# A Mamba-2 output stage with one activation table, its products moved to ScalarE and its exp rows made ahead, and the memory of the later stages laid anew

## Chip, cores and metric

One core of one Trainium2 chip runs the whole layer as one program. The metric is the device time of one execution in microseconds (us). PE is TensorE, DVE VectorE, ACT ScalarE, POOL GpSimd, SP SyncE, which here only issues transfers.

## What is computed

One layer of a diffusion backbone over 1024 latent and 256 context tokens of width 1024, in float32: a normalised input is projected once, and its columns feed latent attention (8 heads), a bidirectional Mamba-2 state-space branch (2048 inner columns, 32 heads of 64, 4 groups of 8 heads, state 128, chunks of 128 tokens), and two gates; then come the merged output projection and a SwiGLU feed-forward network. What the change touches is the end of the Mamba-2 branch:

```
def finish(yf, yb, x_, z_):
    y = (yf + yb + d * x_).reshape(b, -1, D_INNER)
    return rmsnorm(y * jax.nn.silu(z_), w_ssd_norm)
```

`yf` and `yb` are the forward and the backward scan. With cs the running sum of the decay's logarithms, C, B and x of a chunk, and S the state that enters it, each direction gives for a chunk exp(cs) (C S) + ((C B^T) masked, times exp(cs_l - cs_m), times dt) x. The gates are sigmoids of other projected columns.

## The kernel before

Matrix products are made to float32 accuracy: each operand is split into a high part, rounded by ACT, and the rest, by DVE's subtraction, and a 128x512 tile takes three products (L145, L146, L147). The stages are: preparation, the projection of x, B and C with its convolution (the xBC stage, 140 to 535 us in the profile), the end of the reverse scan, the **SSD output stage** (about 590 to 1139 us), attention (to 1608 us), and the output stage with the feed-forward network (to the end). A scheduler orders the instructions of each engine from the program's order, its pools of buffers and its dependences.

The SSD output stage (L693 to L830) works on 32 chunks, 8 for each of 4 groups. For chunk i `load_in` (L697) brings B and C (`bc`) and the rows of cs of both directions, broadcast over the partitions (`cf`, `cb`); `load_out` (L706) the backward state (`sbt`), `ra` with x, and `xz` with d x and silu(z). `in_a` makes the exponent: POOL subtracts a column from `cf` (L721), DVE takes for each of 8 heads the minimum with `cb` less a column (L733), ACT the exp (L735); PE makes C B^T (`pg`), DVE masks it for both directions (`gw`, L726, L727); ACT also makes exp(cs) in four instructions, the upper and the lower half of the partitions apart, as heads lie (`ef`, L742). `in_b` weighs the masks with dt: POOL for the backward direction (`um`, L752), DVE adds the forward one head by head (L757) and multiplies (L758). `out_a` multiplies the states with C (`py`, L771), weighs them (L772), makes the next state (`pst`, L775, and DVE's sum `sn`, L498 in `chunk_state`), adds the directions and d x on POOL (L779, L780), and multiplies with x (`pyd`, L787); `out_b` adds (L794) and multiplies with silu(z) (L795), `chunk_end` stores y (L800). `in_a` runs two chunks ahead of `out_a`, `in_b` one.

Between these, PE is filled with the projection of z and the gates, `zg_steps` (L637 to L665): 32 blocks of 16 steps, each step three products; four blocks come before the stage. 12 steps stand at the stage's start, 13 between the chunks' products (ZG_A to ZG_E), the rest at its end. ACT takes Silu or Sigmoid of a finished block (L655), so that it changes its activation table between these and exp. The weights of each block are split by ACT (L116) and DVE (L117).

Attention's pools are opened over the memory of the stage before, so that its first loads (`ckvh`, `ckvl`, L849) wait for the last users of their place. The output stage begins with y2, the gated y: 16 half tiles are loaded, ACT or DVE rounds them (`load_half`, L1046 to L1054), `sq_add` (L1062) sums their squares on ACT and POOL, and each is split in place, so that the loads hold the buffers of the split (`u`, NU = 80 of 128x512).

Of the kernel before, what the change touches and what calls it, by code (L numbers as in the profile page):

```python
# [54 lines left out]
NU, NW, NE = 80, 20, 4  # L55
# [4 lines left out]
def hybrid_layer(ctx, tc, ins, out):  # L60
# [398 lines left out]
    V.tensor_copy(cs_t[:, :, 0:32], pcf)  # L459
    V.tensor_copy(cs_t[:, :, 32:64], pcb)  # L460
    for q in range(2):
# [77 lines left out]
    with ExitStack() as es:  # L539
# [101 lines left out]
        def zg_steps(pp_tile, zt_tile):  # L641
# [3 lines left out]
            fn = AF.Silu if b < 16 else AF.Sigmoid  # L645
            zt = None
            for hf in range(2):
# [914 lines left out]
```

## Time and profile before

| | us |
|---|---|
| Median of three runs (lowest, highest) | 2654.67 (2651.73, 2655.33) |
| Profiled execution | 2657.29 |
| its span in the trace | 2655.5 |
| SSD output stage, 598 to 1100 | 502 |
| PE busy in the span | 2488.9 (94%) |
| DVE, ACT, POOL busy in the span | 1772.9, 1189.3, 978.9 |

The profiled execution is one run; its span runs from the first to the last instruction. The mean granted clock of PE is 0.975 of full speed. A busy share over the whole span mixes stages with different limits; the rows below are therefore taken from single stages.

### The profile page before, as it was taken

Reading aid. Unit: us, or ns where it says so; the run is one execution under the profiler, and the core shown is the slowest. Engines: PE = TensorE matmul, PEld = TensorE weight load, DVE = VectorE, ACT = ScalarE, POOL = GpSimd, SP = SyncE. Lnnn points to the kernel's source line nnn. Section 1 sums busy time; section 2 is a strip of 40 time slices with the busy share of each in tenths; the row PEclk is TensorE's granted clock in tenths of the full one; section 3 lists DMA queues with packets and bytes.
Section 4 is the critical chain, followed back from the end, with each engine's and each line's share of the span. In section 5 each row is a group of like instructions: output and inputs, shape, how many; then the busy total and the mean of one; then the engine's idle time right before and its main releaser. Section 6 shows DMA issues by size and latency. Waiting matters only on the chain. (4 is left out here: it accounts for less than half of the span.)

```text
span 2655.5 us, 35014 instructions
## 1 busy us (share of the span) xinstructions
PE 2488.9 (94%) x12716; PEld 2039.1 (77%) x12716; DVE 1772.9 (67%) x2715; ACT 1189.3 (45%) x2036; POOL 978.9 (37%) x800
## 2 busy tenths in 40 slices
PE   8999999987888888879999998999999999999998
PEld 5778787766667767768888886888887778888887
DVE  3766767758888888646776866254449655555876
ACT  5633333325656566435666664232235332234443
POOL 1312333346666666533443545271011423222000
PEclk9999999999999999989999997999999999999999
DMA  8455664456766666420000112243351323226713
GB/s 304 131 159 185 210 193 135 151 182 226 232 208 215 209 226 209 146 99 11 17 17 9 43 46 90 84 155 112 126 184 37 120 84 117 106 80 239 278 38 123
DMA packets 241373, 367.41 MB, mean 138 GB/s; under 512 B 17584, under 2 KB 127280, under 8 KB 241200
## 3 DMA queue, kind: packets, MB, share of 16 engines
q1 hardware_dynamic: 206128, 323.22, 36.6%
q10 hardware_dynamic: 35072, 41.95, 4.6%
q8 instruction: 100, 1.64, 0.3%
q14 instruction: 73, 0.60, 0.1%
HBM read 262.87 MB, written 102.24 MB: 137 GB/s over the span
## 5 line engine op out<-in xcount | busy, mean ns | idle before, releaser
L145 PE MATMUL pp<-hTh,whi 128*128 128x512 f32 x896 | 373.2, 417 | 0.0
L145 PE MATMUL pse<-hi 128*128 128x512 f32 x924 | 361.4, 392 | 9.7 <-DVE c L1301 5.3
L147 PE MATMUL pse<-hi,lo 128*128 128x512 f32 x924 | 361.3, 391 | 0.8 <-DVE lo L1036 0.7
L146 PE MATMUL pse<-lo,hi 128*128 128x512 f32 x924 | 361.2, 391 | 0.0
L146 PE MATMUL pp<-hTl,whi 128*128 128x512 f32 x896 | 351.6, 392 | 0.0
L147 PE MATMUL pp<-hTh,wlo 128*128 128x512 f32 x896 | 351.4, 392 | 0.0
L1036 DVE TENSOR_TENSOR lo<-wr,hi 128x512 fp32r<-128x512 f32 x231 | 167.9, 740 | 134.8 <-ACT hi L1035 134.7
L1035 ACT ACTIVATE hi<-wr 128x512 fp32r<-128x512 f32 x231 | 141.0, 627 | 254.4 <-PE pse L146 60.2
L117 DVE TENSOR_TENSOR wlo<-wraw,whi 128x1024 fp32r<-128x1024 f32 (+1 forms) x106 | 153.6, 1450 | 109.3 <-ACT whi L116 102.7
L953 POOL TENSOR_TENSOR prob<-prob,mx 128x1280 f32<-128x1280 f32 x64 | 149.2, 2332 | 209.5 <-DVE mx L952 87.3
L145 PEld LDWEIGHTS pse<-hi 128*128 128x128 f32 x924 | 174.2, 189 | 51.3 <-DVE c L1301 8.7
L146 PE MATMUL pse<-lo,whi 128*128 128x512 f32 x512 | 204.6, 400 | 9.2 <-DVE lo L1053 9.0
L145 PEld LDWEIGHTS pp<-hTh,whi 128*128 128x128 f32 x896 | 169.8, 190 | 51.8 <-issue 18.0
L147 PEld LDWEIGHTS pse<-hi,lo 128*128 128x128 f32 x924 | 174.3, 189 | 38.1 <-DVE lo L1036 2.1
L145 PE MATMUL pse<-hi,whi 128*128 128x512 f32 x512 | 202.1, 397 | 0.9 <-ACT hi L1052 0.5
L147 PE MATMUL pse<-hi,wlo 128*128 128x512 f32 x512 | 202.6, 396 | 0.0
L146 PEld LDWEIGHTS pse<-lo,hi 128*128 128x128 f32 x924 | 174.1, 188 | 36.9 <-DVE lo L1036 1.0
L146 PEld LDWEIGHTS pp<-hTl,whi 128*128 128x128 f32 x896 | 169.8, 189 | 40.2 <-issue 7.8
L733 DVE SCALAR_TENSOR_TENSOR xm<-cb,cs_t,xm 128x128 f32<-128x128 f32 x256 | 180.2, 747 | 26.5 <-POOL xm L721 24.9
L147 PEld LDWEIGHTS pp<-hTh,wlo 128*128 128x128 f32 x896 | 169.0, 189 | 37.2 <-issue 0.3
L116 ACT ACTIVATE whi<-wraw 128x1024 fp32r<-128x1024 f32 (+1 forms) x106 | 111.0, 1048 | 169.5 <-PE pse L146 115.0
L564 DVE SCALAR_TENSOR_TENSOR sv<-u,cols,sv 128x1284 f32<-128x1284 f32 (+1 forms) x96 | 159.3, 1660 | 1.4
(340 smaller groups left out, 5729.2 us busy)
## 6 DMA issues: line engine op xcount, KB each, us to landing
wr<-w_ffn SPq DMA_DIRECT2D x88, 256.0 KB, 3.8
tb<-bt_d SPq DMA_DIRECT2D x77, 256.0 KB, 5.3
wa<-w_ada ACTq DMA_DIRECT2D x64, 256.0 KB, 5.2
wraw<-w_zg SPq DMA_DIRECT2D x32, 512.0 KB, 4.4
cf<-csT_d SPq DMA_DIRECT2D x32, 512.0 KB, 5.4
cb<-csT_d SPq DMA_DIRECT2D x32, 512.0 KB, 3.9
xz<-rb_d SPq DMA_DIRECT2D x32, 512.0 KB, 4.4
ra_d<-xt SPq DMA_DIRECT2D x20, 640.0 KB, 5.2
```

The lines of the kernel that those rows point to most:

```text
L116: S.activation(hi, raw, AF.Copy)
L117: V.tensor_tensor(lo, raw, hi, ALU.subtract)
L145: PE.matmul(ps, lhsT=sh, rhs=mh, start=first, stop=False, skip_group_check=more)
L146: PE.matmul(ps, lhsT=sh, rhs=ml, start=False, stop=False, skip_group_check=more)
L147: PE.matmul(ps, lhsT=sl, rhs=mh, start=False, stop=last, skip_group_check=more)
L564: V.scalar_tensor_tensor(sv[:, 0:nn], u[:, j : j + nn], cw(j), sv[:, 0:nn], ALU.mult, ALU.add)
L733: V.scalar_tensor_tensor(xm[:, a, :], cb[:, h, :], csb[:, h : h + 1], xm[:, a, :], ALU.subtract, ALU.min)
L953: GP.tensor_tensor(pr, pr, mx[:, 6:7].to_broadcast([P, TA]), ALU.mult)
L1035: S.activation(hi, src, AF.Copy)
L1036: V.tensor_tensor(lo, src, hi, ALU.subtract)
```

## The change

The SSD output stage needs one activation table: silu and sigmoid are made from Tanh, which lies in the table of Exp, with a second ACT pass, and for z with a multiply on DVE. Exp(cs) is made once in the xBC stage, stored in HBM, and loaded for each chunk as two broadcasts of 64 partitions (`ld_ef`). The subtraction of `xm` goes from POOL to 8 ACT instructions with a column as bias (cs is kept negated in the forward half for that), the weights `um` from POOL and DVE to 16 ACT instructions with a column as scale and two DVE sums. The store of y comes one chunk later, behind the next loads. The pools of attention are laid in another order; the output stage gets a pool of 16 buffers of its own (`r`), laid first, for raw loads and short-lived tiles, NU goes from 80 to 71, and a smaller scratch for DMA makes room. The splits of the first y2 tiles are no longer in place, and their squares come after them.

```diff
-NU, NW, NE = 80, 20, 4
+NU, NR, NW, NE = 71, 16, 20, 4
...
-    V.tensor_copy(cs_t[:, :, 0:32], pcf)
+    V.tensor_scalar(cs_t[:, :, 0:32], pcf, -1.0, None, ALU.mult)
...
+        ec = p1.tile([64, NT, P], F32, name="ec")
+        def exp_rows(i):
+            if i == 2:
+                SY.dma_start(ec, csT_d.rearrange("c h l -> h c l"))
+            elif i == 4:
+                S.activation(ec, ec, AF.Exp)
+            elif i in (6, 7):
+                di = i - 6
+                for g in range(G):
+                    for v in range(2):
+                        h0 = 32 * di + 8 * g + v
+                        SY.dma_start(ecT_d[:, g, v, di].rearrange("c a l -> a c l"), ec[h0 : h0 + 7 : 2])
...
-                S.activation(zt[:, hs(hf)], pp, fn)
+                S.activation(zt[:, hs(hf)], pp, AF.Tanh, scale=0.5)
+                S.activation(zt[:, hs(hf)], zt[:, hs(hf)], AF.Identity, scale=0.5, bias=halfc)
+                if b < 16:
+                    V.tensor_tensor(zt[:, hs(hf)], zt[:, hs(hf)], pp, ALU.mult)
...
+        def ld_ef(g, t):
+            ef = p2.tile([P, 2, 4, P], F32, tag="ef", name="ef", bufs=3)
+            for v in range(2):
+                SY.dma_start(ef[64 * v : 64 * v + 64], ecT_d[t, g, v].partition_broadcast(64))
+            return ef
...
+            c["ef"] = ld_ef(g, t)
...
-            csf, csb = h8(cs_t, 0, g, t), h8(cs_t, 1, g, t)
+            ncf, csb = h8(cs_t, 0, g, t), h8(cs_t, 1, g, t)
             c["xm"] = [p2.tile([P, 4, P], F32, tag="xm", name="xm", bufs=6) for _ in range(2)]
-            for hh in range(2):
-                h4 = slice(4 * hh, 4 * hh + 4)
-                GP.tensor_tensor(c["xm"][hh], cf[:, h4, :], bc3(csf[:, h4], P), ALU.subtract)
+            for h in range(R):
+                S.activation(c["xm"][h // 4][:, h % 4, :], cf[:, h, :], AF.Identity, bias=ncf[:, h : h + 1])
...
-            ef = p2.tile([P, 2, 2, 2, P], F32, tag="ef", name="ef", bufs=3)
-            for di, c_ in enumerate((cf, cb)):
-                c5 = c_.rearrange("p (a j v) l -> p a j v l", j=2, v=2)
-                for v in range(2):
-                    rs = slice(64 * v, 64 * v + 64)
-                    S.activation(ef[rs, :, di], c5[rs, :, :, v, :], AF.Exp)
-            c["ef"] = ef
...
-            ums = []
             for hh in range(2):
-                um = p2.tile([P, 4, P], F32, tag="um", name="um", bufs=3)
-                GP.tensor_tensor(um, gw[:, 1:2, :].to_broadcast([P, 4, P]), bc3(dtb_[:, 4 * hh : 4 * hh + 4], P), ALU.mult)
-                ums.append(um)
-            for um, xm, hh in zip(ums, c["xm"], range(2)):
+                xm = c["xm"][hh]
+                um, ub = [p2.tile([P, 4, P], F32, tag=n_, name=n_, bufs=2) for n_ in ("um", "ub")]
                 for a in range(4):
                     h = 4 * hh + a
-                    V.scalar_tensor_tensor(um[:, a, :], gw[:, 0, :], dtf[:, h : h + 1], um[:, a, :], ALU.mult, ALU.add)
+                    S.activation(um[:, a, :], gw[:, 0, :], AF.Copy, scale=dtf[:, h : h + 1])
+                    S.activation(ub[:, a, :], gw[:, 1, :], AF.Copy, scale=dtb_[:, h : h + 1])
+                V.tensor_tensor(um, um, ub, ALU.add)
                 V.tensor_tensor(xm, xm, um, ALU.mult)
...
-            chunk_end(i, out_b(i, c))
+            y_i = out_b(i, c)
             if i + 2 < n:
                 load_out(i + 2, cs[i + 2])
             if i + 3 < n:
                 cs[i + 3] = load_in(i + 3)
+            if i > 0:
+                chunk_end(i - 1, y_p)
+            y_p = y_i
             steps(zg, ZG_C)
+        chunk_end(n - 1, y_p)
...
-        pf = pool("pd0", es=es)
-        p3 = pool("pd1", es=es)
-        pv_ = pool("pd2", es=es)
-        pe_ = pool("pd3", es=es)
+        pe_ = pool("pd0", es=es)
+        pf = pool("pd1", es=es)
+        p3 = pool("pd2", es=es)
+        pv_ = pool("pd3", es=es)
...
+        pr4 = pool("per", es=es)
...
+        def split2(raw, fast=False):
+            hi, lo = u("hi", F32R), u("lo", F32R)
             if fast:
-                V.tensor_copy(hi, lo)
+                V.tensor_copy(hi, raw)
             else:
-                S.activation(hi, lo, AF.Copy)
-            V.tensor_tensor(lr, lo, hi, ALU.subtract)
-            return hi, lr
+                S.activation(hi, raw, AF.Copy)
+            V.tensor_tensor(lo, raw, hi, ALU.subtract)
+            return hi, lo
...
-        y2 = [[load_y2(k, 0, raw[k])] for k in range(8)]
+        y2 = [[split2(raw[k])] for k in range(8)]
         for k in range(8):
-            y2[k].append(load_y2(k, 1, raw[8 + k]))
+            y2[k].append(split2(raw[8 + k]))
...
+                if d == 0:
+                    for k in range(8):
+                        sq_add(ssy, hf, raw[8 * hf + k])
...
-    nc = _bacc.Bacc("TRN2", target_bir_lowering=False, num_devices=1)
+    nc = _bacc.Bacc("TRN2", target_bir_lowering=False, num_devices=1, dynamic_dma_scratch_size=1024)
```

The order of DVE in the middle of the third group, one chunk, before (`gw` are the two masked products, `sn` the state, `ef` the weighted states):

```order
L733 SCALAR_TENSOR_TENSOR xm<-cb,cs_t,xm 128x128 x4
L726 TENSOR_TENSOR gw<-pg,msk 128x128
L727 TENSOR_TENSOR gw<-pg,msk 128x128
L733 SCALAR_TENSOR_TENSOR xm<-cb,cs_t,xm 128x128 x2
L757 SCALAR_TENSOR_TENSOR um<-gw,dt_t,um 128x128 x5
L758 TENSOR_TENSOR xm<-xm,um 128x512
L757 SCALAR_TENSOR_TENSOR um<-gw,dt_t,um 128x128 x3
L733 SCALAR_TENSOR_TENSOR xm<-cb,cs_t,xm 128x128
L758 TENSOR_TENSOR xm<-xm,um 128x512
L772 TENSOR_TENSOR ef<-ef,py 128x512 x2
L733 SCALAR_TENSOR_TENSOR xm<-cb,cs_t,xm 128x128
L498 TENSOR_TENSOR sn<-sn,pst 128x512
```

and with the change:

```order
L758 TENSOR_TENSOR gw<-pg,msk 128x128
L759 TENSOR_TENSOR gw<-pg,msk 128x128
L765 SCALAR_TENSOR_TENSOR xm<-cb,cs_t,xm 128x128 x8
L121 TENSOR_TENSOR wlo<-wraw,whi 128x1024
L796 TENSOR_TENSOR ef<-ef,py 128x2x256 x2
L780 TENSOR_TENSOR um<-um,ub 128x512
L504 TENSOR_TENSOR sn<-sn,pst 128x512
L781 TENSOR_TENSOR xm<-xm,um 128x512
```

The eight small sums of `um` are gone, two large ones stand in their place, and the eight minima stand together.

The order of PE at the start of the last group, where `sf` is that group's first state (`pp` are products of z and the gates), before:

```order
L146 MATMUL pp_8666<-hTl_247,whi 128x512
L147 MATMUL pp_8666<-hTh_239,wlo 128x512
L771 MATMUL py<-bc,sf 128x128 x2
L771 MATMUL py<-bc,sbt 128x128 x2
L771 MATMUL py<-bc,sf 128x128 x2
L771 MATMUL py<-bc,sbt 128x128 x2
L775 MATMUL pst<-xw,ra 128x512
L145 MATMUL pp_8666<-hTh_240,whi 128x512
```

and with the change:

```order
L151 MATMUL pp_9287<-hTh_239,wlo 128x512
L149 MATMUL pp_9287<-hTh_240,whi 128x512
L150 MATMUL pp_9287<-hTl_248,whi 128x512
L794 MATMUL py<-bc,sf 128x128 x2
L794 MATMUL py<-bc,sbt 128x128 x2
L794 MATMUL py<-bc,sf 128x128 x2
L794 MATMUL py<-bc,sbt 128x128 x2
L799 MATMUL pst<-xw,ra 128x512
L151 MATMUL pp_9287<-hTh_240,wlo 128x512
L794 MATMUL py<-bc,sn 128x128 x2
L794 MATMUL py<-bc,sbt 128x128 x2
L794 MATMUL py<-bc,sn 128x128 x2
```

The first `py` of the group (on `sf`) is followed, with the change, by that of its second chunk (on `sn`), with no product of `pp` between; the products that stood there have moved ahead of the first one.

The order of ACT at the start of the output stage, before:

```order
L979 ACTIVATE ob<-po 128x256
L980 DMA oT_d_134<-ob 128x256
L1066 ACTIVATE sqa<-lo 128x512
L1069 ACTIVATE sq<-lo 128x512
L1052 ACTIVATE hi<-lo 128x512
L1069 ACTIVATE sq<-lo 128x512 x2
L1052 ACTIVATE hi<-lo 128x512
```

and with the change:

```order
L1007 ACTIVATE ob<-po 128x256
L1008 DMA oT_d_135<-ob 128x256
L1083 ACTIVATE hi<-raw 128x512 x16
L1155 ACTIVATE acc<-pse 128x512
L1102 ACTIVATE sqa<-raw 128x512
L1105 ACTIVATE sq<-raw 128x512 x8
```

All 16 roundings (`hi`) now stand ahead of the squares (`sqa`, `sq`), which before stood between them.

## Rows read from the trace of the kernel before

**Rows 1.** Windows, 598 to 1100 us. Columns: window, its us, busy us (instructions) of PE, PEld, DVE, ACT, POOL, clock, DMA share, GB/s.

```profile
598.00:1100.00 502.00, 427.46 (x2268) 336.90 (x2267) 435.25 (x767) 293.86 (x359) 321.67 (x269) 0.94 0.64 212
```

**Rows 2.** One tile's instructions, yt: the stores of y on SP.

```profile
L800 SPq DMA_DIRECT2D y_d<-yt x32: 370/370/371, 632.5 to 1122.6; - x32
```

**Rows 3.** Timeline of PE, 919 to 928 us. Columns: start us, us, instruction.

```profile
919.86 0.68 PE L771 MATMUL py<-bc,sn 128*128 128x128 f32 x4 [0.93 <-DVE sn L498]
...
922.18 0.79 PE L145 MATMUL pp<-hTh,whi 128*128 128x512 f32 x1
922.81 0.39 PE L146 MATMUL pp<-hTl,whi 128*128 128x512 f32 x1
923.03 0.39 PE L147 MATMUL pp<-hTh,wlo 128*128 128x512 f32 x1
...
926.77 1.09 PE L787 MATMUL pyd<-xm,ra 128*64 128x128 f32 x16
```

**Rows 4.** Waits, 598 to 1100 us. Columns: us in total, times, longest.

```profile
ACT xm L735 <- DVE xm L733: 133.7, 44, 7.3
...
PE py L771 <- DVE sn L498: 56.4, 24, 4.7
...
DVE xm L733 <- POOL xm L721: 24.9, 21, 1.3
```

**Rows 5.** Timeline of DVE, 907 to 917 us.

```profile
907.85 2.94 DVE L733 SCALAR_TENSOR_TENSOR xm<-cb,cs_t,xm 128x128 f32<-128x128 f32 x4 [1.31 <-POOL xm L721]
...
916.71 0.34 DVE L733 SCALAR_TENSOR_TENSOR xm<-cb,cs_t,xm 128x128 f32<-128x128 f32 x1
```

**Rows 6.** Groups of instructions, 598 to 1100 us: count | busy us, mean ns | idle before, releaser.

```profile
L733 DVE SCALAR_TENSOR_TENSOR xm<-cb,cs_t,xm 128x128 f32<-128x128 f32 x256 | 180.2, 747 | 26.5 <-POOL xm L721 24.9 <-DMA cb<-csT_d 1.6
...
L757 DVE SCALAR_TENSOR_TENSOR um<-gw,dt_t,um 128x128 f32<-128x128 f32 x248 | 105.1, 481 | 0.0
...
L758 DVE TENSOR_TENSOR xm<-xm,um 128x512 f32<-128x512 f32 x62 | 43.8, 706 | 0.0
...
L721 POOL TENSOR_TENSOR xm<-cf,cs_t 128x512 f32<-128x512 f32 x64 | 71.2, 1132 | 17.2 <-DMA cf<-csT_d 17.2
...
L752 POOL TENSOR_TENSOR um<-gw,dt_t 128x512 f32<-128x512 f32 x62 | 65.7, 1079 | 31.3 <-DVE gw L726 27.8 <-DVE xm L758 3.5
```

**Rows 7.** The same view: ScalarE.

```profile
L655 ACT ACT_TABLE_LOAD x47 | 60.3, 1283 | 3.8 <-DMA rb_d<-zt 3.0
...
L742 ACT ACT_TABLE_LOAD x30 | 38.5, 1283 | 7.4 <-DMA cf<-csT_d 4.2 <-ACT zt L655 2.8
...
L735 ACT ACT_TABLE_LOAD x18 | 23.1, 1283 | 50.0 <-DVE xm L733 49.9
...
L742 ACT ACTIVATE ef<-cf 64x512 f32<-64x512 f32 x64 | 40.2, 628 | 9.2 <-DVE yt L794 8.6
```

**Rows 8.** Timeline of ScalarE, 88.9 to 90.2 us: small shapes.

```profile
88.99 0.30 ACT L317 ACTIVATE junkb<-mt 128x128 f32<-128x128 f32 x1
89.19 0.19 ACT L317 ACTIVATION_READ_ACCUMULATOR junkb<-mt 128x1 f32 x1
...
90.18 0.55 ACT L262 ACTIVATE hf<-pt,modt,a 128x256 f32<-128x256 f32 x1
```

**Rows 9.** The page's part 2: bytes moved in 40 slices of 66.4 us.

```profile
GB/s 304 131 159 185 210 193 135 151 182 226 232 208 215 209 226 209 146 99 11 17 17 9 43 46 90 84 155 112 126 184 37 120 84 117 106 80 239 278 38 123
```

**Rows 10.** Timeline of PE, 1139 to 1144 us.

```profile
1143.19 0.79 PE L146 MATMUL pk<-ckvl,whi 128*128 128x512 f32 x1 [3.91 <-DMA ckvl<-mq_dl]
```

**Rows 11.** Windows, 1610 to 1640 us.

```profile
1610.00:1640.00 30.00, 23.06 (x51) 13.89 (x52) 26.91 (x23) 12.44 (x24) 20.88 (x14) 0.54 0.25 88
```

**Rows 12.** Timeline of DVE and POOL from 1609 us.

```profile
1609.68 0.69 DVE L1053 TENSOR_TENSOR lo<-lo,hi 128x512 fp32r<-128x512 f32 x1 [1.19 <-ACT sqa L1066]
...
1611.73 3.45 DVE L1053 TENSOR_TENSOR lo<-lo,hi 128x512 fp32r<-128x512 f32 x2
...
1610.25 21.82 POOL L1070 TENSOR_TENSOR sqa<-sqa,sq 128x512 f32<-128x512 f32 x14 [8.14 <-ACT sq L1069]
```

More of the change, by code (lines that the diff above doesn't have):

```diff
@@ L102, in hybrid_layer @@
     V.memset(epsc, EPS)
+    halfc = cp.tile([P, 1], F32, name="halfc")
+    V.memset(halfc, 0.5)
     modt = cp.tile([P, 6, KD, 2], F32, name="modt")
@@ L465, in hybrid_layer @@
         S.activation(dec_t[:, sl5], ptt, AF.Exp)
-        V.tensor_tensor(wst_t[:, sl5], ptt, cs_t[:, sl5], ALU.subtract)
+        V.tensor_tensor(wst_t[:, sl5, 0:32], ptt[:, :, 0:32], cs_t[:, sl5, 0:32], ALU.add)
+        V.tensor_tensor(wst_t[:, sl5, 32:64], ptt[:, :, 32:64], cs_t[:, sl5, 32:64], ALU.subtract)
     S.activation(wst_t, wst_t, AF.Exp)
@@ L473, in hybrid_layer @@
         cst = bp.tile([64, 4, P], F32, tag="cst", name="cst", bufs=1)
-        V.tensor_copy(cst, pct)
+        V.tensor_scalar(cst[0:32], pct[0:32], -1.0, None, ALU.mult)
+        V.tensor_copy(cst[32:64], pct[32:64])
         SY.dma_start(csT_d[q * 4 : q * 4 + 4].rearrange("c h l -> h c l"), cst)
@@ L626, in hybrid_layer @@
             pps = xbc_mm(b)
+            exp_rows(i)
             steps(scan, 1)
@@ L771, in out_a @@
                         PE.matmul(py[:, di, j, :], lhsT=st_[:, jj * P : jj * P + P], rhs=cT, start=True, stop=True)
-                V.tensor_tensor(ef[:, hh], ef[:, hh], py, ALU.mult)
+                e_ = ef[:, :, 2 * hh : 2 * hh + 2, :]
+                V.tensor_tensor(e_, e_, py, ALU.mult)
             if t < NT - 1:
@@ L776, in out_a @@
                 sf = chunk_state(g, t, 0, sf, pst)
-            e0, e1 = ef[:, :, 0], ef[:, :, 1]
+            e0, e1 = ef[:, 0], ef[:, 1]
             steps(zg, ZG_D)
             GP.tensor_tensor(e0, e0, e1, ALU.add)
-            GP.tensor_tensor(e0, e0, xz[:, 0:512].rearrange("p (a j l) -> p a j l", j=2, l=P), ALU.add)
+            GP.tensor_tensor(e0, e0, xz[:, 0:512].rearrange("p (a l) -> p a l", l=P), ALU.add)
             pyd = ps2.tile([P, 4, P], F32, tag="pyd", name="pyd", bufs=1)
@@ L792, in out_b @@
         def out_b(i, c):
-            yt = p2.tile([P, 2, 2, P], F32, tag="yt", name="yt", bufs=2)
-            V.tensor_tensor(yt, c["ef"][:, :, 0], c["pyd"].rearrange("p (a j) l -> p a j l", j=2), ALU.add)
-            GP.tensor_tensor(yt, yt, c["xz"][:, R_SZ - R_XD : RB_N - R_XD].rearrange("p (a j l) -> p a j l", j=2, l=P), ALU.mult)
-            return yt.rearrange("p a j l -> p (a j) l")
+            yt = p2.tile([P, 4, P], F32, tag="yt", name="yt", bufs=3)
+            V.tensor_tensor(yt, c["ef"][:, 0], c["pyd"], ALU.add)
+            GP.tensor_tensor(yt, yt, c["xz"][:, R_SZ - R_XD : RB_N - R_XD].rearrange("p (a l) -> p a l", l=P), ALU.mult)
+            return yt
         def chunk_end(i, yt):
@@ L1028, in u, with r @@
             return p4.tile([P, 512], dt, tag="u", name=name, bufs=NU)
+        def r(name, dt=F32):
+            return pr4.tile([P, 512], dt, tag="r", name=name, bufs=NR)
         def ps():
@@ L1039, in fetch, with load_half, load_y2 @@
         def fetch(src, hf):
-            lr = u("lo", F32R)
-            SY.dma_start(lr.bitcast(F32), src[:, hs(hf)])
-            return lr
-        def load_half(src, hf, sums=None, fast=False, lr=None):
-            lr = lr if lr is not None else fetch(src, hf)
-            hi, lo = u("hi", F32R), lr.bitcast(F32)
-            if sums is not None:
-                sq_add(sums, hf, lo)
+            t_ = r("raw")
+            SY.dma_start(t_, src[:, hs(hf)])
+            return t_
+        def split2(raw, fast=False):
+            hi, lo = u("hi", F32R), u("lo", F32R)
             if fast:
-                V.tensor_copy(hi, lo)
+                V.tensor_copy(hi, raw)
             else:
-                S.activation(hi, lo, AF.Copy)
-            V.tensor_tensor(lr, lo, hi, ALU.subtract)
-            return hi, lr
+                S.activation(hi, raw, AF.Copy)
+            V.tensor_tensor(lo, raw, hi, ALU.subtract)
+            return hi, lo
+        def load_half(src, hf):
+            return split2(fetch(src, hf))
         def y2_src(k):
             return y2_d[k // 4][k % 4]
-        def load_y2(k, hf, lr=None):
-            return load_half(y2_src(k), hf, ssy, k < 8 and k % 2 == 0, lr)
+        def load_y2(k, hf):
+            raw = fetch(y2_src(k), hf)
+            sq_add(ssy, hf, raw)
+            return split2(raw)
         def sq_add(sums, hf, src, eng=None):
@@ L1105, in gate @@
         def gate(k):
-            return [ld("gt", gT_d[k][:, hs(hf)]) for hf in range(2)]
+            return [ld("gt", gT_d[k][:, hs(hf)], r) for hf in range(2)]
         ssy = [None, None]
@@ L1299, in post @@
                 elif i == 5:
-                    st[5] = u("c22")
+                    st[5] = r("c22")
                     V.tensor_tensor(st[5], st[7], b, ALU.add)
```

14 lines of the change are left out of this document (7 added, 7 removed).

## The prediction

> **What bounds the kernel now.** I read the windows first, since the change lies almost wholly in one stage. From 598 to 1100 us [rows 1] PE is busy 427.5 of 502 us, DVE 435.3, ACT 293.9, POOL 321.7; the clock is 0.94. No engine is full, so the next view is the rhythm: 32 y stores from 632.5 to 1122.6 [rows 2], 490.1 / 31 = 15.81 us a chunk. The windows then give for each chunk (502 / 15.81 = 31.75 of them): DVE 13.7 us, PE 13.5, POOL 10.1, ACT 9.3, the DMA engines 0.64 x 15.81 = 10.1 with 212 GB/s x 15.81 = 3.35 MB.
>
> The PE timeline [rows 3] shows what a chunk costs PE at full clock: py and pst from 919.86 to 922.18 = 2.32; the first product's successor starts 0.63 later, where a later one starts 0.22 to 0.23 later (+0.40); 39 products at 0.23 = 8.97; pyd 1.09; for pg and the slower products around it and pyd I add 0.3. Sum 13.1. So of 15.81 PE loses 2.7, and the row that begins py says to whom: it waited for DVE's state sum. The waits [rows 4] say it for the stage: 56.4 us in 24 waits of py on `sn`. DVE's timeline [rows 5] shows why the sum can be late: it stands last of the chunk's row in DVE's order, and ahead of that row DVE stood still for 1.31 us until POOL had made `xm`; all such waits are 24.9 us [rows 4], 0.8 a chunk. The stage is bound by DVE (13.7 and about 2.1 of waits), with PE 2.7 behind.
>
> **The change, part by part.** *Sums of um.* DVE loses 248 instructions of L757, 105.1 us [rows 6], 3.3 a chunk, and gains two sums of 128x512 a chunk; the nearest row is the product L758 of the same shape, 0.706, so +1.4. *xm and um leave POOL.* POOL loses 71.2 + 65.7 us [rows 6], 4.3 a chunk, and keeps 5.8. DVE's minimum instruction L733 takes 0.747 on the mean, but 0.34 where it stands alone at 916.71 [rows 5]: 256 x 0.407 = 104 us, 3.3 a chunk, are not its own work. I charge them to POOL, and as POOL keeps 5.8 of 10.1, I let 1.9 stay and take off 1.4. *z's multiply.* 12 of the 28 blocks made here get two multiplies; by L758 again, 24 x 0.706 = 17 us, 1.1 in each of the first 15 chunks. DVE comes to 13.7 - 3.3 + 1.4 - 1.4 = 10.4, and 11.5 early. Bounds: 8.5 if all excess goes; 8.5 + 5.8 = 14.3, plus 0.5 for z on the mean, if each us of POOL's that is left stops DVE.
>
> *ACT.* It loses 94 of 95 table loads of 1.283 [rows 7], 3.8 a chunk, and the 128 instructions for `ef`, 64 from `cf` in 40.2 us [rows 7] and as many of the same shape from `cb`, 2.5 a chunk: 9.3 leaves 3.0. It gains 24 instructions of 128x128 with a column as factor or summand. No such row is there; the nearest are the square of 128x128 at 88.99, 0.30 long, whose successor starts 0.20 later, and the 128x256 with two columns, 0.55 [rows 8]. I take 0.30, as the shape is the same: 7.2; bounds 0.20 and 0.55, so 4.8 and 13.2. The second pass over z, 48 by the 0.628 of `ef` [rows 7], adds 0.9. ACT comes to 11.1 in the period: busier than before, below PE. [...] Before the change ACT waits 133.7 us for DVE's minimum [rows 4], so ACT's new work at the head of the chain (xm) and in its middle (um) lies beside DVE's of other chunks, two chunks ahead. If ACT fell behind, DVE's minimum, then exp, pyd and y would be late.
>
> *DMA.* `ef` comes by two broadcasts, 0.52 MB: 3.87 MB a chunk, 11.7 us of DMA time where it was 10.1. Covered by the period; the first slice of the program moved 304 GB/s [rows 9], where this needs 3.87 MB in 14.4 us, 269. SP issues two more rows a chunk. The y store goes behind the loads, and belongs to the chunk before, so SP waits no longer for POOL's last multiply with loads queued behind it; the price is a third `yt`. I cost that at nothing: the stage's long waits are on engines [rows 4], so loads come in time, and a chunk of 14.4 us hides them. If that cover went, `sf` of a new group, now issued behind them, would be late, three times, and py with it.
>
> *New period.* DVE 10.4 to 11.5, ACT 11.1, DMA 11.7, PE 13.1: PE becomes the bound. The 0.8 for POOL's xm goes; of the other 1.3 of the 2.1 I keep all, now as PE's waits for the state: 14.4. Less than 1.3 would mean that the clock drops after waits also vanish (at 0.94 they are in PE's 13.5 already), more that DVE's new order is no better. Gain (15.81 - 14.4) x 31 = **44 us**; bounds for the period 13.5 and 15.2.
>
> *The entry to attention.* PE stands for 3.91 us at 1143.19 for `ckvl` [rows 10], loaded only after the last z product, as its place is in use until then. In the order of the change the first loads wait for no engine. **-4**, bounds 0 and -6.
>
> *The entry to the output stage.* From 1610 to 1640 [rows 11] PE does 51 matmuls in 30 us at a clock of 0.54. At 0.23 they are 11.7, so 18 are lost. DVE's row there is two `lo` in 3.45 us, 1.72 each, where the first, just before POOL's first sum, took 0.69 [rows 12]; POOL adds squares for 21.82 us on end. After the change the 16 splits read tiles that are loaded ahead, stand before the squares, and POOL's sums come after. **-15**; bounds -5 (loads late) and -18. [...]
>
> *The xBC stage.* One exp over 64x1024, one load and 16 stores; no table load is added. **+1**, 0 to +4. FFN: 71 buffers and 16 for other use, taken at **0**, +-5; PE is covered there by tiles split ahead.
>
> Sum -44 - 4 - 15 + 1 = -62. The profiled execution took 2657.3 (span 2655.5): 2595.3. It stands 2.6 above the median of the three runs, 2654.7, so against that: **2593**. With the good ends (13.5: -72 - 6 - 18) it is 2559, with the bad (15.2: -19 + 0 - 5 + 4) 2635.
>
> **Rivals.** *PE's order at the groups.* Where a new group's `sf` is needed, the changed order has 31 z steps ahead of its first py instead of 13. If those 18 steps (18 x 3 x 0.23 = 12.4 us) run while DVE has nothing, and later chunks then lack products to fill PE, three groups lose 37 us: 2593 + 37 = 2630. For: the order itself. Against: it moves products, and adds none; DVE has work two chunks ahead. Chance 0.10.
>
> *POOL stops DVE for all of its time.* DVE 14.3 + 0.5 and 1.3 of waits: 16.1, +9 for the stage, with -18 for the rest: 2646. For: `lo` at 1.72. Against: 104 us of L733 excess in a stage where POOL works 321.7, a third. Chance 0.06. [...]
>
> *Slower: ACT becomes the bound.* If one of the 24 column instructions costs as much as the 128x256 row, 0.55, ACT needs 13.2 + 3.0 + 0.9 = 17.1 and, with 1.3 of waits, 18.4: +80 in the stage, -18 elsewhere, 2717. It decides from 0.465 on: 24 x 0.465 + 3.0 + 0.9 + 1.3 = 16.4, +18, which eats the 18 gained outside. For: 24 instructions in a chain that DVE and PE wait for; ACT's queue is in order, so a z pass behind them holds a PSUM buffer. Against: the row of 128x128. Chance 0.09.
>
> *Slower: DMA.* If 0.64 is all that this pattern of packets gets, 11.7 / 0.64 = 18.3: +77 - 18, 2714. Against: the first slice. Chance 0.05. That the table loads stay is excluded by the order: it holds one in the stage.
>
> **How the numbers follow.** Forecast 0.70, rivals 0.10, 0.06, 0.09, 0.05. The time is the forecast's, 2593. The range 2555 to 2640 takes its own bounds and the first rival, and leaves 0.2 outside, the three other rivals. About 0.2% (5.3 us) is what can be told from no change. The first three cases are faster, 0.86, of which 0.03 (the rivals' far ends) falls within that bound; the last two slower, 0.14. So faster 0.83, same 0.03, slower 0.14.
>
> **What would show it.** y stores 14.4 us apart (13.5 to 15.2); DVE near 10.9 of each chunk, L765 well under 0.747; ACT near 11, its column instructions at 0.30 from start to start; py's waits for `sn` near half of 56.4 us, the clock above 0.94; under 2 us before the first pk products; the first 51 matmuls of the output stage in about 15 us. Wrong if the distance of stores stays at 15.8 or above; then the row ahead of py, or DVE's row ahead of the minimum, names whether POOL, ACT or a load took the place.

## The result and the profile after

The changed kernel takes **2574.3 us** (median of four runs, 2572.5 to 2578.1), the one before 2653.2 in the same comparison: a ratio of 0.9707, 95% interval 0.9689 to 0.9725. The forecast was 2593, its range 2555 to 2640.

The gain stands at fixed events of the two traces (starts on PE or DVE; the span's end):

| event | before | after | gained since the event above |
|---|---|---|---|
| first sum of y (DVE) | 629.4 | 619.1 | 10.3 |
| last sum of y | 1120.5 | 1056.5 | 53.7 |
| first `pk` product, attention | 1138.8 | 1073.7 | 1.1 |
| first product with y2, output stage | 1608.5 | 1532.2 | 11.2 |
| last product with y2 | 1985.2 | 1901.2 | 7.7 |
| end of the span | 2655.5 | 2573.5 | -2.0 |

The second and the third row of the table come from one tile's instructions, `yt`, the sums of y (`pk` are attention's first products, `pse` below those of the output stage; durations least, median, most; first and last start), after and before:

```profile
L818 DVE TENSOR_TENSOR yt<-ef,pyd x32: 672/676/689, 619.1 to 1056.5; 128x512 f32<-128x512 f32 x32
```

```profile
L794 DVE TENSOR_TENSOR yt<-ef,pyd x32: 668/675/690, 629.4 to 1120.5; 128x512 f32<-128x512 f32 x32
```

437.4 / 31 = 14.11 us a chunk, where it was 491.1 / 31 = 15.84. From the first to the last of these sums, before and after (columns as in [rows 1]):

```profile
629.40:1120.50 491.10, 423.41 (x2266) 335.41 (x2265) 423.87 (x746) 280.94 (x342) 318.52 (x263) 0.94 0.63 209
```

```profile
619.10:1056.50 437.40, 409.69 (x2289) 324.50 (x2289) 344.61 (x593) 334.12 (x917) 204.10 (x146) 0.98 0.86 272
```

PE is idle for 67.7 us before and for 27.7 after. That is 40.0 of the 53.7 us; the other 13.7 are PE's own time, at a granted clock of 0.98 in place of 0.94. The windows of the stage after (columns as in [rows 1]):

```profile
598.00:1058.00 460.00, 427.13 (x2374) 337.99 (x2374) 357.58 (x619) 350.07 (x962) 210.28 (x151) 0.97 0.87 272
```

460 / 14.11 = 32.6 chunks: PE 13.1, DVE 11.0, ACT 10.7, POOL 6.5 us each, and the DMA engines 0.87 x 14.11 = 12.3. PE is busy for 93% of the stage, where [rows 1] gives 85%. Its waits on other work there (us, times, longest):

```profile
PE pg L756 <- DMA bc<-rb_d: 21.8, 12, 4.1
PE pyd L811 <- DVE xm L781: 2.8, 5, 0.9
PE py L794 <- DVE sn L504: 2.1, 2, 1.9
```

The state that PE waited 56.4 us for [rows 4] now comes in time; what is left is a load. The groups that answer to [rows 6, 7]:

```profile
L778 ACT ACTIVATE um<-gw,dt_t 128x128 f32<-128x128 f32 x256 | 99.6, 389 | 10.5 <-DVE gw L759 8.8 <-DVE zt L680 0.6 <-issue 0.3
...
L765 DVE SCALAR_TENSOR_TENSOR xm<-cb,cs_t,xm 128x128 f32<-128x128 f32 x256 | 88.0, 405 | 18.5 <-DMA cb<-csT_d 10.1 <-ACT xm L753 7.9
...
L781 DVE TENSOR_TENSOR xm<-xm,um 128x512 f32<-128x512 f32 x64 | 72.5, 1133 | 1.3
L780 DVE TENSOR_TENSOR um<-um,ub 128x512 f32<-128x512 f32 x64 | 67.2, 1052 | 25.2 <-ACT ub L779 24.5
...
L767 ACT ACT_TABLE_LOAD x1 | 1.3, 1283 | 0.0
```

One table load of 1.283 us stands in the stage, where there were 95 [rows 7]; the Tanh and Exp behind it need no second. The minima fell from 747 to 405 ns. The 128x512 instructions L780 and L781, two operands in SBUF each, take 1.05 and 1.13 us where L758 took 0.706. Sorted by whether an instruction of POOL runs at the same time, L781 takes 677 to 694 ns in 27 cases without one and 1458 ns on the mean in 37 beside one; the minima take 0.34 without one, in both kernels, and 1.01 (before) and 0.90 (after) beside one. So what POOL costs DVE has partly moved to the large instructions. L796, of the same shape with one operand in PSUM (`py`), takes 671 to 690 ns in all 64 cases, 16 of them beside POOL (durations as above):

```profile
L781 DVE TENSOR_TENSOR xm<-xm,um x64: 677/1044/1791, 614.9 to 1046.8; 128x512 f32<-128x512 f32 x64
```

```profile
L796 DVE TENSOR_TENSOR ef<-ef,py x64: 671/679/690, 611.2 to 1052.2; 128x512 f32<-128x512 f32 x64
```

One ACT instruction with a column as bias or factor shows 389 ns, but eight stand in 2.43 us, 0.29 from start to start:

```profile
851.99 2.43 ACT L753 ACTIVATE xm<-cf,cs_t 128x128 f32<-128x128 f32 x8
```

At the entry to the output stage the window that answers to [rows 11] has 126 matmuls in 30 us at full clock, where there were 51 at 0.54; ACT makes the 16 high parts and DVE the 16 low ones, 0.61 us each, in one go:

```profile
1532.00:1562.00 30.00, 29.55 (x126) 23.55 (x127) 17.90 (x22) 25.41 (x48) 19.55 (x13) 1.00 0.61 206
```

```profile
1531.54 8.44 ACT L1083 ACTIVATE hi<-raw 128x512 fp32r<-128x512 f32 x16 [0.40 <-ACT ob L1007]
```

```profile
1532.20 9.72 DVE L1084 TENSOR_TENSOR lo<-raw,hi 128x512 fp32r<-128x512 f32 x16 [4.08 <-ACT hi L1083]
```

And yet the stretch of products with y2 is only 7.7 us shorter. The PE timeline inside it, at full clock and without a wait, before and after, shows why:

```profile
1650.16 0.39 PE L145 MATMUL pse<-hi,whi 128*128 128x512 f32 x1
1650.39 0.39 PE L146 MATMUL pse<-lo,whi 128*128 128x512 f32 x1
1650.62 0.39 PE L147 MATMUL pse<-hi,wlo 128*128 128x512 f32 x1
1650.84 0.39 PE L145 MATMUL pse<-hi,whi 128*128 128x512 f32 x1
```

```profile
1574.81 0.40 PE L149 MATMUL pse<-hi,whi 128*128 128x512 f32 x1
1575.05 0.39 PE L150 MATMUL pse<-lo,whi 128*128 128x512 f32 x1
1575.28 0.40 PE L151 MATMUL pse<-hi,wlo 128*128 128x512 f32 x1
1575.52 0.39 PE L149 MATMUL pse<-hi,whi 128*128 128x512 f32 x1
```

Three products take 0.68 us before and 0.71 after. Over all neighbouring products with y2 that start 0.21 to 0.25 us apart the mean is 0.2268 before and 0.2333 after; over the later ones of the stage 0.2269 and 0.2311. In the xBC stage it is 0.2274 and 0.2275. Something made PE 2 to 3% slower in one stage, at the same granted clock: 1536 x 0.0065 = 10 us with y2, and 2772 x 0.0042 = 12 in the rest, unless waits hide it.

### The profile page after: what moved, and what is told of

Its sections match the earlier page's. It is cut to its first block, busy times and chain, and to the rows that moved or that the text cites. A ratio compares the mean times of both kernels' runs of the same rounds, so it can differ in the third digit from the quotient of the medians.

```text
span 2573.5 us, 35225 instructions
## 1 busy us (share of the span) xinstructions
PE 2472.4 (96%) x12716; PEld 2017.8 (78%) x12716; DVE 1666.1 (65%) x2552; ACT 1252.0 (49%) x2653; POOL 858.4 (33%) x672
## 5 line engine op out<-in xcount | busy, mean ns | idle before, releaser
L121 DVE TENSOR_TENSOR wlo<-wraw,whi 128x1024 fp32r<-128x1024 f32 (+1 forms) x106 | 146.0, 1378 | 110.2 <-ACT whi L120 92.3
L149 PEld LDWEIGHTS pp<-hTh,whi 128*128 128x128 f32 x896 | 171.5, 191 | 49.9 <-issue 15.4
L993 ACT ACTIVATE pth<-ptp 128x512 fp32r<-128x512 f32 (+1 forms) x192 | 100.1, 527 | 91.4 <-PE ptp L991 89.3
```

What stands on the lines that cost most here:

```text
L121: V.tensor_tensor(lo, raw, hi, ALU.subtract)
L149: PE.matmul(ps, lhsT=sh, rhs=mh, start=first, stop=False, skip_group_check=more)
L993: S.activation(dh, pt[:, 0:n, :], AF.Copy)
```

## The experiments

### Why products in the output stage are slower

The new constant `halfc` takes 32 bytes of each partition, and every pool laid from the left starts 32 bytes later. In the programs' memory maps the moving tiles of the output stage start at 96 past a multiple of 128 bytes before, at 0 after; the weights, laid from the right, at 96 in both. A third of the later products has both operands in a pool laid from the right. Four kernels change only that.

**Shared column** (x1): the two constants in one tile.

```diff
-    epsc = cp.tile([P, 1], F32, name="epsc")
-    halfc = cp.tile([P, 1], F32, name="halfc")
+    epsh = cp.tile([P, 2], F32, name="epsh")
+    epsc, halfc = epsh[:, 0:1], epsh[:, 1:2]
```

> The changed kernel with the two constants, eps and one half, in one 128x2 tile in place of two 128x1 tiles. Nothing else changes; every pool laid from the left then starts 32 bytes lower, so that the moving tiles of the output stage start at 32 past a multiple of 64 again, as in the kernel before. Theory (address): in the changed kernel products of the output stage start 0.2333 us apart (1536 of them with y2, until 1895 us) and 0.2312 (2772 later ones) where before they started 0.2267 and 0.2269 apart, because the moving tile starts at 0 and the weights at 32 past a multiple of 64. Then the distance is 0.2267 again and the time falls by 1536 x 0.0066 + 2772 x 0.0043 = 22 us, to 2552. Rival (buffers): the products are slower for another reason, as the separate raw and split buffers or the writes of DVE beside them; then the distance stays and the time stays at 2574 (within 4).

**Unused tile in the kernel before** (x2):

```diff
     V.memset(epsc, EPS)
+    unused = cp.tile([P, 1], F32, name="unused")
+    V.memset(unused, 0.5)
```

> The kernel before with one more constant tile of 128x1 that nothing reads. Theory (address): every pool laid from the left moves up by 32 bytes, the products of the output stage with y2 start 0.2333 us apart, later ones 0.2311, and the time rises by 1536 x 0.0066 + 2772 x 0.0043 = 22 us, to 2675. Rival (buffers): the distance stays at 0.2267 and the time at 2653 (within 4).

**Unused tile from the right**, in the changed kernel (x3) and in the one before (x4):

```diff
     esW = ExitStack()
+    rp = pool("rpad", side="right")
+    rpad = rp.tile([P, 1], F32, name="rpad")
+    V.memset(rpad, 0.5)
```

> The changed kernel with a tile of 128x1 laid first from the right, which nothing reads: the weights then start at 0 past a multiple of 64, as the moving tiles do in the output stage. Theory (address, mismatch): what costs is that the two operands start in different halves of 64 bytes; now both start at 0, the distance is 0.2267 and the time about 2552. Second theory (address, moving at 0): a moving tile at 0 costs by itself; the distance stays 0.2333, and as all 4308 products of the output stage now have their moving tile at 0, the time rises by 924 x 0.0066 = 6 us to 2580. In the xBC stage the moving and the weight tiles are both laid from the right and move together: by the first theory their distance stays 0.2267, by the second it becomes 0.2333, and with some 2700 products there and in z's the time comes to about 2598. Rival (buffers): no change, 2574.

> The kernel before with a tile of 128x1 laid first from the right, which nothing reads: in the output stage the moving tiles start at 32 and the weights at 0 past a multiple of 64 (a third of the later products has both at 0). Theory (mismatch): distance 0.2333 with y2, 0.2311 later, time up by 22 us, 2675. Second theory (moving at 0): distance 0.2267 with y2 and 0.2289 later, while the xBC stage and z's products, whose moving tiles now start at 0, go to 0.2333, so that about 2688 x 0.0066 = 18 us come on top there. Rival (buffers): no change.

| kernel | moving tile, weights: start past a multiple of 128 bytes | distance with y2, later | ratio to before [95%] |
|---|---|---|---|
| before | 96, 96 | 0.2268, 0.2269 | 1 |
| changed | 0, 96 | 0.2333, 0.2311 | 0.9707 [0.9689, 0.9725] |
| x1 | 96, 96 | 0.2268, 0.2269 | 0.9648 [0.9620, 0.9676] |
| x2 | 0, 96 | 0.2333, 0.2311 | 1.0047 [1.0030, 1.0064] |
| x3 | 0, 64 | 0.2289, 0.2282 | 0.9668 [0.9647, 0.9690] |
| x4 | 96, 64 | 0.2333, 0.2311 | 1.0063 [1.0041, 1.0084] |

The PE timeline of x1, to be held against the two above: 0.68 for three again.

```profile
1700.12 0.39 PE L150 MATMUL pse<-lo,whi 128*128 128x512 f32 x1
1700.35 0.39 PE L151 MATMUL pse<-hi,wlo 128*128 128x512 f32 x1
1700.58 0.39 PE L149 MATMUL pse<-hi,whi 128*128 128x512 f32 x1
1700.80 0.39 PE L150 MATMUL pse<-lo,whi 128*128 128x512 f32 x1
```

The address is shown: one unused tile of four bytes slows the kernel before, and taking one away speeds the changed kernel. The buffers are out, and so is "a moving tile at 0": in x4 the moving tile stays at 96 and the products are as slow, and attention's products `sA`, with both operands at 96 before and both at 0 after, keep 0.2315. In x3 and x4 the xBC stage's products, whose two operands moved together, keep 0.2275. My first theory, in halves of 64 bytes, missed x3, where I expected 0.2267. All six kernels fit if the *difference* of the two starts counts, moving less weights, in 128 bytes: 0 gives 0.2268, 64 gives 0.2289, 32 gives 0.2333. (The later products mix two thirds of that with one third at 0.2268: 0.2311 and 0.2282, as measured.) That reading was made after the fact, but one execution bears it out: with the memory map held against the changed kernel's trace, product by product, neighbouring later products with both starts alike are 0.2267 apart (917 distances), those with the starts 32 apart 0.2333 (1812). The price in time was smaller than expected, 15.6 us between the changed kernel and x1 by the ratios (22 expected), 12.5 for x2 and 16.7 for x4; only the interval of x2, 8 to 17 us, leaves 22 clearly out. The products with y2 pay 8 to 10 of 10: their stretch is 376.6 before and 386.1 in x2, 368.9 changed and 360.9 in x1. The later ones pay 4 to 5 of 12 (from there to the last of them 653.8 and 659.2, 656.9 and 652.8): where products are faster, PE waits more there, 11.3 us for DVE and ACT in x1 and 5.6 in the changed kernel.

### Which part of the change gives the stage's gain

From here on all kernels contain the shared column, and are compared with x1: 2560 us, 13.85 us a chunk.

**Products back on POOL and DVE** (x5):

```diff
-            for h in range(R):
-                S.activation(c["xm"][h // 4][:, h % 4, :], cf[:, h, :], AF.Identity, bias=ncf[:, h : h + 1])
+            for hh in range(2):
+                h4 = slice(4 * hh, 4 * hh + 4)
+                GP.tensor_tensor(c["xm"][hh], cf[:, h4, :], bc3(ncf[:, h4], P), ALU.add)
...
-                    S.activation(um[:, a, :], gw[:, 0, :], AF.Copy, scale=dtf[:, h : h + 1])
-                    S.activation(ub[:, a, :], gw[:, 1, :], AF.Copy, scale=dtb_[:, h : h + 1])
-                V.tensor_tensor(um, um, ub, ALU.add)
+                    V.scalar_tensor_tensor(um[:, a, :], gw[:, 0, :], dtf[:, h : h + 1], um[:, a, :], ALU.mult, ALU.add)
```

> The kernel with the shared constant tile, with xm and um made as before the change (POOL's subtraction and weighting, eight DVE instructions); tables, exp rows, stores and memory as changed. Theory (DVE was the bound and the products free it): DVE takes 11.0 us of a chunk in the changed kernel (78% of 14.1); with 3.3 for the eight instructions more, 2.1 for the two sums less, and 8 x (0.747 - 0.405) = 2.7 for the minima beside POOL more, it needs 14.9, the distance of y goes from 13.85 to about 15.2, and the time rises by 31 x 1.3 = 40 us, to about 2600. Rival (ACT's table loads were what held the chunk): they are gone here, so the distance stays at or under 14.2 and the time within 12 us of 2560.

Measured 2640.4, ratio 0.9944 [0.9926, 0.9961]: 80 us more than x1, twice the expected 40. The sums of y stand 16.3 us apart. One window and two groups:

```profile
640.00:1040.00 400.00, 335.74 (x1770) 261.77 (x1770) 352.09 (x626) 95.06 (x145) 243.89 (x209) 0.93 0.77 233
```

```profile
L782 DVE SCALAR_TENSOR_TENSOR um<-gw,dt_t,um 128x128 f32<-128x128 f32 x197 | 127.6, 702 | 33.5 <-POOL um L777 33.5
L766 DVE SCALAR_TENSOR_TENSOR xm<-cb,cs_t,xm 128x128 f32<-128x128 f32 x200 | 85.4, 494 | 2.1 <-DMA cb<-csT_d 2.1
```

ACT is nearly empty (24%), and the stage is slower than in the kernel before (15.84): taking tables and exps off ACT, with the products left where they were, gives nothing. DVE is at 88%, with L782 at 702 ns, where the same instruction was 481 before [rows 6], and DVE now waits for POOL ahead of it; with that wait it is at 96%. A chunk has 14.3 us of DVE, 3.3 more than in x1, of which 2.5 are time beside POOL above the 0.34 and 0.69 that such instructions take alone. So DVE's part came as expected (14.9), and what doubles the price are waits. The moved products free DVE, from its own sums and, more, from POOL; the two were not taken back one by one. The rival that the table loads held the chunk falls.

**Exp rows back on ACT** (x6):

```diff
-            c["ef"] = ld_ef(g, t)
...
+                for v in range(2):
+                    rs = slice(64 * v, 64 * v + 64)
+                    S.activation(ef[rs, di], c5[rs, :, v, :], AF.Exp)
```

> The kernel with the shared constant tile, with exp(cs) made by four ACT instructions a chunk as before, without the exp rows in HBM and their loads; all else as changed. Theory (loads are the wait that is left): PE's longest wait is now 18 us for bc, the DMA engines work at 0.83 to 0.92; without 0.52 MB a chunk their share falls to about 0.73, the wait goes, and the time changes by -15 to 0. Rival (ACT would be full): ACT has 10.9 of 13.85 us; with 2.5 more it needs 13.4, and with its waits the distance rises to 14.5, the time by 20.

Measured 2613.1, ratio 0.9847 [0.9824, 0.9870]: 53 us slower, 15.4 a chunk. PE no longer waits for `bc`, but ACT was the dearer place, as the rival says, and by far more than it priced:

```profile
640.00:1040.00 400.00, 358.35 (x1890) 276.14 (x1889) 242.99 (x494) 342.16 (x874) 151.69 (x122) 0.95 0.68 219
```

```profile
PE pst L805 <- POOL xw L494: 32.6, 17, 4.0
```

ACT is busy for 86%, not for all, so the 53 are not its work alone: PE waits for POOL's `xw`, and POOL for y's sum, 131.7 us. The scheduler has ordered this kernel anew; how much of the 53 is the order was not separated.

**Silu and Sigmoid back** (x7), three lines:

```diff
-                S.activation(zt[:, hs(hf)], pp, AF.Tanh, scale=0.5)
...
+                S.activation(zt[:, hs(hf)], pp, AF.Silu if b < 16 else AF.Sigmoid)
```

> The kernel with the shared constant tile, with Silu and Sigmoid as before in place of Tanh, the second pass and the multiply, so that the table loads are back (74 in the program in place of 12); all else as changed. Theory (the loads cost now, as ACT carries the products): ACT gets 62 x 1.28 = 79 us more and 48 x 0.6 = 29 us less, 1.6 us a chunk, comes to 12.5 of 13.85 and has a load in the chain to exp; the distance rises to about 14.5, the time by 20 us. Rival (table loads lie beside other work): no change within 5 us, or a gain of some us as 24 DVE multiplies go.

Measured 2579.5, ratio 0.9716 [0.9685, 0.9746]: 19 us slower, 14.45 a chunk, as the theory has it. With the products on ACT, which is busy for 339.4 us from 640 to 1040, its table loads (1.283 us each in the kernel before) are no longer hidden.

**y stored in its own chunk** (x8):

```diff
-            y_i = out_b(i, c)
+            chunk_end(i, out_b(i, c))
...
-            if i > 0:
-                chunk_end(i - 1, y_p)
-            y_p = y_i
```

> The kernel with the shared constant tile, with y stored in its own chunk ahead of the next loads, as before. Theory (SP): the store waits for POOL's last multiply and the loads of bc, cf, cb and ra stand behind it in SP's queue, so PE's wait for bc, now 18 us in 11 waits, doubles and more; the time rises by 15 to 30 us. Rival (the loads are late through the DMA engines or their buffers, not through SP's order): the time stays within 5 us.

Measured 2547.8, ratio 0.9593 [0.9565, 0.9622]: 12 us *faster* than x1, against the theory and the rival. The later store costs time. SP's waits in x1, then in x8, 640 to 1040 us:

```profile
SPq L720 <- DMA rb_d<-zt: 70.4, 8, 9.8
SPq L720 <- POOL yt L819: 49.2, 15, 8.7
SPq L720 <- DMA gT_d<-zt: 23.8, 7, 5.4
```

```profile
SPq L824 <- POOL yt L819: 167.7, 29, 9.0
SPq L720 <- DMA rb_d<-zt: 12.5, 6, 5.1
...
SPq L720 <- DMA gT_d<-zt: 7.4, 2, 5.7
```

In x1 the store (L824) no longer waits for POOL, but now the loads (L720) do, since `xz` needs the buffer that POOL's multiply reads, and they wait for stores of z. With the store back, a load lands 5.8 us after its issue in place of 6.8 (medians), and PE's wait for `bc` is 8.2 instead of 18.3, x1 first:

```profile
PE pg L756 <- DMA bc<-rb_d: 18.3, 11, 4.1
```

```profile
PE pg L756 <- DMA bc<-rb_d: 8.2, 4, 3.7
```

The two intervals only just touch.

**A third buffer for xz** (x12), on x1, to tell the two waits apart: `ld("xz", ...)` with 3 buffers.

> The kernel of x1 (shared constant tile, y stored one chunk later) with three buffers in place of two for xz, so that its load waits for POOL's multiply of the chunk one earlier. Theory (POOL's wait moved in SP's queue): in x1 the store of y no longer waits for POOL, but the load of xz does, 49 us in 15 waits, and bc, cf and cb stand behind it; with the wait gone, PE's wait for bc falls from 18 us to about 8, as in x8, and the time to about 2548. Rival (SP's waits for transfers of z on the same queue, 70 us in 8 waits, hold the loads): these stay, the time stays within 4 us of 2560.

Measured 2562.9, ratio 0.9660 [0.9643, 0.9677]: no gain. The loads wait 3.5 us for POOL in place of 49.2, and longer for z's stores, 119.1 us in place of 94.2:

```profile
SPq L720 <- DMA rb_d<-zt: 78.6, 9, 9.9
SPq L720 <- DMA gT_d<-zt: 40.5, 8, 7.9
```

So what separates x1 from x8 goes with the loads' waits for z's stores (`rb_d<-zt`, `gT_d<-zt`), 94.2 us there and 19.9 in x8, not with their waits for POOL. Why a load waits for a store of z no run shows.

### The starts of groups, and the two entries

In the changed kernel the two distances of y's sums around each new group are 25.1 + 5.9, 29.4 + 7.5 and 23.1 + 9.0; the other 25 are 13.5 on the mean. The excess is 99.9 - 6 x 13.5 = 19 us. The next expectation takes such an excess for a loss. The windows of the three pairs show that most of it is work:

```profile
720.26:751.19 30.93, 30.70 (x165) 24.54 (x166) 21.27 (x41) 25.85 (x75) 12.13 (x11) 0.95 0.90 278
834.93:871.84 36.91, 33.05 (x169) 26.35 (x170) 25.34 (x41) 25.61 (x70) 16.41 (x12) 0.91 0.78 257
951.66:983.72 32.06, 29.93 (x173) 23.81 (x171) 24.52 (x51) 24.82 (x71) 15.17 (x11) 1.00 0.82 261
```

PE is idle for 6.2 of these 99.9 us. Counted by their starts, 268 products of z and the gates lie in the six distances, where six of the other 25 hold 221 on the mean; the 47 more are 11 us at 0.23 each, and the other distances are short because they lack them. **The state `sf` loaded two chunks ahead** (x9), on x8:

```diff
+            if t == 0:
+                c["sf"] = sc.tile([P, 512], F32, tag="sf", name="sf", bufs=1)
+                SY.dma_start(c["sf"], sf_d[g])
             c["ef"] = ld_ef(g, t)
...
-                SY.dma_start(sf, sf_d[i // NT])
+                sf = c["sf"]
```

> The kernel of x8 (shared constant tile, y stored in its own chunk) with the first state of a group loaded two chunks ahead, with the other loads of its chunk, in a tile of its own. In the order PE then has 39 products between the py of all chunks, also at a group's start, where it had 97, 86 and 83 and then 7 to 31. Theory (the groups' starts cost): in x8 the two distances of y around a group's start are 29.9, 34.8 and 30.0 us together, where two others take 25.6; the excess, 18 us, goes, and the time falls to about 2530. Rival (the products done early are only moved, and come back as shorter chunks elsewhere, or another load takes the wait): the time stays within 5 us of 2548.

Measured **2536.3**, ratio 0.9556 [0.9532, 0.9581]: 11.5 us faster than x8 by the medians, 10 by the ratios, whose intervals overlap; the lowest median of this study. Pairs around a group's start are 24.3, 33.7 and 26.6, together 10 us less than in x8, but the other 25 distances rise by 5, as the rival has it. From the first to the last sum of y, x8 and then x9:

```profile
624.70:1040.30 415.60, 403.25 (x2295) 321.23 (x2296) 333.98 (x592) 333.33 (x918) 206.90 (x146) 0.99 0.88 287
```

```profile
621.50:1032.30 410.80, 401.51 (x2291) 320.78 (x2291) 336.99 (x592) 333.51 (x917) 206.93 (x146) 0.99 0.89 290
```

PE is busy for 97% and 98%; x9 saves 4.8 us there, not 18. The other 7.6 of the 12.4 us between the two profiled executions lie ahead of the chunks and behind them, where x9 changes nothing, so the theory is borne out at most in part.

**Attention's pools in the old order** (x10), on x8: the four `pool("pd..")` lines as before.

> The kernel of x8 with attention's four pools in the order of the kernel before. Theory (place): the first loads of attention again lie over tiles in use until the last z product, PE waits about 4 us for them and its clock is low after, the time rises by 4 to 11 us (the stretch from pk to y2's first product is 463 us in x8 and 470 in the kernel before). Rival: the entry gains only from the earlier end of ACT and DVE work; no change, within 4 us.

Measured 2557.5, ratio 0.9635 [0.9620, 0.9649]: 10 us slower. From `pk` to y2's first product it takes 469.4 us, as the kernel before (469.8), and 461.5 in x8. PE waits again for `ckvl`, and for `cq` as well, 1.6 to 1.8 us each, and the second window after the entry has the lower clock that the kernel before had. x10, then x8:

```profile
1106.00:1156.00 50.00, 47.90 (x303) 42.84 (x304) 31.54 (x63) 28.18 (x64) 18.41 (x9) 0.93 0.03 9
```

```profile
1106.00:1156.00 50.00, 49.96 (x337) 44.97 (x336) 32.60 (x67) 31.29 (x72) 17.77 (x8) 1.00 0.03 11
```

**Squares ahead of the splits** (x11), on x8:

```diff
-        y2 = [[split2(raw[k])] for k in range(8)]
+        y2 = []
         for k in range(8):
+            sq_add(ssy, 0, raw[k])
+            y2.append([split2(raw[k])])
```

> The kernel of x8 with the squares of the first 16 y2 halves made ahead of each split, as before the change; the loads into tiles of their own, ahead, stay. Theory (POOL beside DVE): POOL's sums again run beside DVE's splits, lo takes 1.7 us, PE gets its operands late and its clock falls; the entry of the output stage loses 15 to 18 us, 2565. Rival (the gain came from the early loads and the splits on ACT alone): the time rises by under 5 us.

Measured 2558.9, ratio 0.9637 [0.9619, 0.9655]: 11 us slower, less than the 15 to 18 expected. The low parts stand beside POOL's sums again and take 1.61 us each, 0.61 in the changed kernel:

```profile
1528.63 19.36 DVE L1080 TENSOR_TENSOR lo<-raw,hi 128x512 fp32r<-128x512 f32 x12
```

The stretch with y2 is 370.7 us, 360.9 in x8. The other 6 us up to the 376.6 of the kernel before lie with what x11 keeps, the loads into tiles of their own; they were not taken away alone.

## Why the prediction was right, and where it was not

The direction and its cause are shown: DVE, with POOL beside it, was the bound of the stage, and the moved products are what frees it (x5). That they need the tables away from ACT is shown too (x7); that they need the exps away is likely, as x6 has an order of its own. Point by point:

- **DVE 10.4 to 11.5 a chunk**: 11.0. The minima gave more than I took off (0.405 in place of some 0.57), the sums and products took more (1.05 and 1.13 in place of 0.706). POOL's price stayed near the 1.9 that I left, 8 x 0.065 + 2 x (0.36 + 0.45) = 2.1 above 0.34 and 0.69, but on other instructions. The trace of the changed kernel shows on which: L780 and L781, with two inputs in SBUF, take 1.18 and 1.46 us on the mean beside POOL and 0.69 each without it; L796, with one of its two in PSUM, takes 0.68 in both cases. The rival in which every us of POOL stops DVE falls.
- **ACT 11.1**: 10.7; a column instruction 0.30: 0.29. The rival "ACT becomes the bound" falls for the change as it is, but x6 shows how near it lay: 2.5 us more a chunk, in an order made anew, and 53 us are gone. Leaving these adds and multiplies on DVE and POOL costs 80 us (x5).
- **DMA 11.7 us a chunk**: 12.3 at 272 GB/s. That 0.64 was no limit is shown, 0.87 was reached, and the rival falls. "Costed at nothing" does not quite hold: PE's longest wait is now for `bc`, 21.8 us.
- **The period, 14.4**: 14.11, and the term that was mis-sized is the 1.3 us of PE's waits for the state. They went almost wholly (56.4 to 2.1); PE is idle for 27.7 / 31 = 0.9 us a chunk, mostly for `bc`. PE's own part, 409.7 / 31 = 13.2, is near the 13.1. The rival of the groups' starts, priced at 37 us, fell for the most part: the order did move the products, but PE is idle for only 6.2 us around the three starts, and x9 saves 5 in the chunks.
- **The y store "at nothing"**: the step that failed. It costs 12 us (x8): SP's wait went from the store to the loads, which also wait for z's stores.
- **The way into the stage, +1**: -10.3. The last product of the reverse scan is 3.5 us earlier (585.9, 582.4), and the first eight minima, 5.84 us beside POOL before, took 2.4. Neither was tried alone, and single executions scatter here: the first sum of y starts at 618.8 to 627.5 us in the three kernels with the changed stage as it is (the changed kernel, x1 and x3) and at 624.8 to 631.4 in the three with the stage as before (the kernel before, x2 and x4). How much of the 10.3 is the change's stays open.
- **The entry to attention, -4**: 11.2 to y2's first product; the clock came back later than I priced (0.93 in the second window before, 1.00 after). x10 puts the pools' part at 10, 8 of them in this stretch.
- **The entry to the output stage, -15**: right. With the distance of products as before, x1 and x8 both make that stretch 15.7 us shorter. The changed kernel keeps 7.7 of it, as its products are slower.
- **The feed-forward part, 0 within 5**: -2, for a reason that I did not see, the 32 bytes.

So the forecast of 2593 lay 19 us above, in its range. By the events of the first table: chunks 9.7 more than I had, the way in 11.3, up to y2's first product 8.3 (1.1 + 11.2 against 4); less at the stretch with y2, 7.3, and behind it 2.0. Together 20, by one execution of each kernel.

That the number came so near is in part luck. Two costs that I did not have, the 32 bytes (2574 against 2560 in x1) and the later store (12 more, x8), took the time up towards the forecast; without them it is 2548, 45 us under the forecast and below the range.

## What to carry to other kernels

Find the engine that bounds the stage, and count what the engine beside it costs it (here L781 takes 0.69 us without POOL and 1.46 beside it): moving its work to another engine paid here, 80 us by x5, where that engine had room, and the room had to be made first (x7, with the table loads back, loses 19 us). When a wait is taken out of a queue, run that reordering by itself: the wait can come back at another instruction (x1 against x8), or as another (x12: 45.7 us less for POOL, 24.9 more for z's stores). An uneven rhythm is not a loss as such: count the work and the idle time in it before pricing it. And after a change of memory, compare the distance of matmuls in stages that the change did not mean to touch.

## What was not expected of the hardware

In the traces of these six kernels the distance of the output stage's 128x512 products (fp32r) goes with where the two operands start in SBUF: 0.2268 us when both start at the same place in 128 bytes (the kernel before, x1), 0.2289 at 64 apart (x3), 0.2333 at 32 apart (the changed kernel, x2, x4), at one granted clock and with no wait. A constant of four bytes, laid first, is enough (x2: 0.2268 to 0.2333). Only these three differences of one shape were seen, and why it is so was not tried.
